# Attention: five of eight diagonal masks put into copies of the gates, and K's low halves gathered in one tile

## The chip, the cores and the metric

The kernel runs on one core of one Trainium2 chip. The metric is device time in microseconds (us) of the whole program. Six things work side by side: TensorE (PE in the profile, with its weight loads shown apart as PEld), VectorE (DVE), ScalarE (ACT), GpSimd (POOL), SyncE (SP), which issues the loads and stores, and the DMA engines that carry them out.

## What is computed

A trunk of two layers over a sequence of 1024 rows of width 1024 in float32. The first layer mixes rows by attention with forgetting gates, the second by gated linear attention, and each is followed by a SwiGLU block. The change touches only the attention of the first layer:

```python
log_f = jax.nn.log_sigmoid(f_logit + b_f)
cum = jnp.cumsum(log_f, axis=1).transpose(0, 2, 1)
scale = FOX_HEAD_DIM ** -0.5
for blk in range(S // Q_BLOCK):                       # 8 blocks of 128 queries
    qs, qe = blk * Q_BLOCK, (blk + 1) * Q_BLOCK
    logits = jnp.einsum('bqhd,bkhd->bhqk', q[:, qs:qe], k[:, :qe]) * scale
    logits = logits + cum[:, :, qs:qe, None] - cum[:, :, None, :qe]
    mask = (qs + jnp.arange(Q_BLOCK))[:, None] >= jnp.arange(qe)[None, :]
    logits = jnp.where(mask[None, None], logits, -jnp.inf)
    p = jax.nn.softmax(logits, axis=-1)
    outs.append(jnp.einsum('bhqk,bkhd->bqhd', p, v[:, :qe]))
```

There are 16 heads of width 64. `cum` is the running sum of the gates' logarithms: each key column carries its own value, and the query's own value drops out in the softmax. In a block of 128 queries only the last 128 keys, the diagonal block, hold pairs to be masked.

## The kernel before

**Layout.** Float32 precision is rebuilt on TensorE from operands split in a high part (float32r, rounded) and a low part (the rest). A projection `mm3` (lines 304 to 307) is three products: high by high, high by low, low by high. Weights stand in the array in tiles of 128 rows by 128 columns, and up to 512 columns stream past them.

**Scores.** Heads go in eight pairs `p`, with `a` = 0 or 1 inside a pair; head h is 2p + a. A unit `(p, a, g)` is one head and two query blocks of 128, qb = 2g and 2g + 1. `scores` (line 1261) does a unit: for each query block it cuts the keys up to the diagonal into one or two parts of at most 512 columns (`cuts`: one part for qb 0 to 3, two for qb 4 to 7), 12 parts in a head. For each part there are

- L1281: a product of Q (128 partitions: the 64 high rows and the 64 low rows, negated and scaled) with K's high half, which stands twice, on both halves of the partitions,
- L1282: a product of the same Q tile with K's low half, which stands on 64 partitions; the other 64 partitions of its tile are zero, so that only Q's high rows count,
- L1284, only for the part that holds the diagonal block: an identity times `maskb` (bf16, 128x128, 1e30 above the diagonal, 0 elsewhere), added into the last 128 columns of the same sum.

The sums stand in PSUM, in one of two buffers (`sr`). DVE then adds the gates' row and takes the minimum in one pass (L1287; signs are turned, so a masked pair is a large positive number). After the parts of a query block ACT takes the exponential with its sum (L1291), DVE the reciprocal (L1292), and POOL scales the rows (L1293). Three tiles per head hold K: `KA` and `KB` (high halves) and `KLA` or `KLB` (low half of the head a = 0 or 1 with its 64 zero partitions).

**Evacuation of K.** `k_evac` (line 863) runs for each half of 512 columns: POOL writes the zeros (L866, L867), ACT makes four copies of the high halves (L868 to L871), DVE subtracts twice for the low halves (L872, L873).

**Gates.** `cum` goes to DRAM once (L1094). `load_cum(h)` (L1106 to L1108) broadcasts a head's row of 1024 values to 128 partitions, into one of two buffers. The first two are loaded in the prologue (`gates_end`), and two more at the end of each pair (L1389, L1390).

**Outputs and order.** `outputs` (line 1296) transposes the scaled rows (L1313), splits them (ACT L174, DVE L175) and multiplies by V (L1325, L1327). A unit's outputs come one unit later than its scores. Within a head the units go in `ORDER` = g 0, 3, 1, 2. While a pair is worked on, `weave` (line 130) threads the next pair's Q and K projections, and half of a group of V, between the scores and outputs by planned costs, and keeps PE's order of the two strands with a lag of 18 yields; after the seventh pair the output projection takes that place. Other steps run in the gaps: weight splits on ACT, POOL and DVE (L242, L246), and the modulation vectors, accumulated on DVE (L505) and POOL (L466, L468) from loads that SP issues (L442). SP works its queue in order: a load that has to wait for its buffer holds up all that stand behind it, the weights (L227) among them.

**Before attention**, in the first microseconds, vectors are turned into columns by transposes of 32, 8 and 16 rows (L1115 and L416) among transposes of 128 rows (L630, L413). In the second layer L331 transposes 128 rows of 16 columns.

**Slots.** SBUF is handed out in slots of 4 KB per partition. The tiles of Q and K take nine: eight, and the slot `s1_sl`, which the prologue uses for modulation weights.

The functions that the change touches:

Of the kernel before, what the change touches and what calls it, by code (L numbers as in the profile page):

```python
# [9 lines left out]
F32 = mybir.dt.float32  # L10
# [43 lines left out]
def trunk(ctx, tc, x, c, ada_w, ada_b, norm1_g, norm2_g, ffn_w_in, ffn_w_out,  # L54
# [768 lines left out]
    vring = Ring(big, take(8))  # L823
    qk_free = deque(take(8) + s1_sl)
    qk_all = list(qk_free)
# [14 lines left out]
    def qk_tiles(p):  # L840


        at = {nm: qk_free.popleft() for nm in ("QA", "QB", "KA")}
        if p:
            before = qk_at.pop(p - 1)
            at.update(zip(("KB", "KLA", "KLB"), (before[nm] for nm in ("QA", "KA", "KLA"))))
            qk_free.extend(before[nm] for nm in ("QB", "KB", "KLB"))
        else:
            at.update({nm: qk_free.popleft() for nm in ("KB", "KLA", "KLB")})
        qk_at[p] = at  # L850
        return {nm: big.tile([P, S], FR, tag=sl, name=f"{nm}{p}") for nm, sl in at.items()}
# [11 lines left out]
    def k_evac(ps, t, hf):  # L863
        cs = hsl(hf)
        KA, KB, KLA, KLB = t["KA"], t["KB"], t["KLA"], t["KLB"]
        nc.gpsimd.memset(KLA[64:128, cs].bitcast(F32), 0.0)  # L866
        nc.gpsimd.memset(KLB[0:64, cs].bitcast(F32), 0.0)  # L867
        nc.scalar.copy(KA[0:64, cs], ps[0:64, :])  # L868
        nc.scalar.copy(KB[64:128, cs], ps[64:128, :])
        nc.scalar.copy(KA[64:128, cs], ps[0:64, :])  # L870
        nc.scalar.copy(KB[0:64, cs], ps[64:128, :])  # L871
        nc.vector.tensor_sub(KLA[0:64, cs], ps[0:64, :], KA[0:64, cs].bitcast(F32))  # L872
        nc.vector.tensor_sub(KLB[64:128, cs], ps[64:128, :], KB[64:128, cs].bitcast(F32))  # L873

# [216 lines left out]
    def gates_end():  # L1091
# [3 lines left out]
        load_cum(0)  # L1095
        load_cum(1)

    def v_split(g, tp, ps):
# [5 lines left out]
    cums = {}  # L1104

    def load_cum(h):  # L1106
        cums[h] = cumr([P, S], F32, f"cum{h}")
        nc.sync.dma_start(cums[h], cum_d[h].partition_broadcast(P))  # L1108

# [151 lines left out]
    def scores(u):  # L1261

        p, a, g = u
        t = qkt[p]
        Qs, K1, KL = (t["QA"], t["KA"], t["KLA"]) if a == 0 else (t["QB"], t["KB"], t["KLB"])
        cm = cums[2 * p + a]
        if g < 2:
            both = lpr([P, (4 * g + 3) * P], F32, f"lp{p}{a}{g}")
# [4 lines left out]
        for qi in range(2):  # L1273
# [3 lines left out]
            for n_, (k0, k1) in enumerate(zip(cuts, cuts[1:])):  # L1277
# [3 lines left out]
                nc.tensor.matmul(ps, Qs[:, qs], K1[:, k0:k1], start=True, stop=False)  # L1281
                nc.tensor.matmul(ps, Qs[:, qs], KL[:, k0:k1], start=False, stop=not diag)  # L1282
                if diag:
                    nc.tensor.matmul(ps[:, k1 - k0 - P:], identb, maskb, start=False, stop=True)  # L1284
                mnew = st[:, qi, n_:n_ + 1]
                with tc.issue_after(v_last) if early else ExitStack():
                    nc.vector.tensor_tensor_reduce(lp[:, k0:k1], ps, cm[:, k0:k1], 1.0, mcur,  # L1287
                                                   ALU.add, ALU.min, mnew)
# [67 lines left out]
    def attention(p):  # L1356
        for a in range(2):
            for g in ORDER:
                u = (p, a, g)
                lps = yield from scores(u)  # L1360
                if p:
                    ada0p(0.8)
# [19 lines left out]
    in_order(begin)  # L1382
    v_last = last_of("D")
    for p in range(7):
        parts = [qk_proj(p + 1, 0), qk_proj(p + 1, 1)]
        if p < 6:
            parts.insert(1, v_half(p // 2 + 1, p % 2))
        weave(attention(p), 23.0, chain(*parts), 31.0 if p < 6 else 20.8, LAGS)
        load_cum(2 * p + 2)  # L1389
        load_cum(2 * p + 3)  # L1390
    ada0.flush()
# [1157 lines left out]
```

## Time and profile before

| | |
|---|---|
| median of 3 runs | 2350.84 us (2349.58 to 2350.93) |
| profiled execution, its own time | 2349.75 us |
| span of its instructions | 2348.0 us |
| mean granted clock of TensorE | 0.995 |
| PE, DVE, ACT, POOL busy, us | 2327.2, 1778.5, 1123.2, 1141.2 |
| products and weight loads | 12168 each |
| first and last product of scores (L1281) start | 97.6 and 589.1 us |
| mask products (L1284) | 128 |

A busy time is the union of recorded durations. Matmuls overlap in the records, since one starts while the one ahead still drains, and their ends are modelled; so the time that a product costs in PE's stream is read from the distance between starts in the timeline. A row of the timeline gives the start, the duration, the engine, the line, the operation, output<-inputs, the weights' size (rows * columns), the shape and type of what streams, how many were merged (x), and in brackets the idle time ahead of it and what ended it. A row of the table by stretches gives a stretch and its length, then the busy time (and count) of PE, PEld, DVE, ACT and POOL, the granted clock, the DMA share and GB/s. In a list of waits stand the waiting line, the line waited for, the total in us, the times and the longest.

### The profile page before, as it was taken

How to read it: one execution, taken by the hardware profiler on the slowest of the kernel's cores; microseconds unless marked ns; L12 is line 12 of the kernel's file. 1: busy time of each engine (PE TensorE's matmuls, PEld its weight loads, DVE VectorE, ACT ScalarE, POOL GpSimd, SP SyncE). 2: the span in 40 equal slices, each digit the busy share in tenths (PEclk: the TensorE clock that was granted, in tenths of full speed). 3: DMA queues.
4: the chain of work that ended last, by engine and by line, in shares of the span. 5: the costliest groups of instructions: out<-in, count | busy, mean ns of one | idle time of the engine just before them, and what ended most of it. 6: DMA issues, size and time to landing. Idle time of an engine off the chain costs nothing.

```text
span 2348.0 us, 35560 instructions
## 1 busy us (share of the span) xinstructions
PE 2327.2 (99%) x12168; PEld 1984.9 (85%) x12168; DVE 1778.5 (76%) x2947; ACT 1123.2 (48%) x2166; POOL 1141.2 (49%) x1005
## 2 busy tenths in 40 slices
PE   8999999999999999999999999999999999999999
PEld 7988888888888888888888899898888888888888
DVE  6578787877688888886788666568787777876787
ACT  6566565675443333344325654345444333345236
POOL 1334445533345656665563522345456666664651
PEclk8999999999999999999999999999999999999999
DMA  8423333332325545458774443555434544458674
GB/s 264 146 77 116 108 115 94 125 129 102 117 95 188 184 162 171 156 174 314 252 270 154 136 127 99 151 171 171 141 111 157 178 149 157 139 188 300 237 264 140
DMA packets 349614, 383.38 MB, mean 163 GB/s; under 512 B 25372, under 2 KB 286648, under 8 KB 349432
## 3 DMA queue, kind: packets, MB, share of 16 engines
q1 hardware_dynamic: 349432, 381.11, 49.4%
q8 instruction: 96, 1.57, 0.3%
q14 instruction: 86, 0.70, 0.1%
HBM read 279.76 MB, written 101.25 MB: 162 GB/s over the span
## 4 chain that ended last, share of the span: by engine, by line
PE 88%; DVE 4%; DMA 3%; issue 1%; ACT 1%; POOL 1%; SPq 1%; DVEq 0%; POOLq 0%; ACTq 0%
PE p_b L305 16%; PE p_b L307 16%; PE p_b L306 16%; PE o_b L1327 2%; PE t_b L1313 2%; PE qk_b L305 2%; PE qk_b L306 2%; PE qk_b L307 2%; PE vps_b L307 1%; PE vps_b L305 1%; PE vps_b L306 1%; PE gv_b L305 1%; PE gv_b L307 1%; PE gv_b L306 1%; PE gr_b L305 1%
## 5 line engine op out<-in xcount | busy, mean ns | idle before, releaser
L174 ACT CAST o_s<-xv_s 128x512 fp32r<-128x512 f32 (+1 forms) x392 | 236.3, 610 | 340.1 <-PE p_b L307 254.3
L175 DVE TENSOR_TENSOR o_s<-xv_s,o_s 128x512 fp32r<-128x512 f32 (+1 forms) x392 | 335.6, 861 | 43.2 <-ACT o_s L174 42.6
L307 PE MATMUL p_b<-B,o_s 128*128 128x512 f32 x608 | 236.0, 389 | 0.0
L306 PE MATMUL p_b<-B,o_s 128*128 128x512 f32 x608 | 235.9, 389 | 0.0
L305 PE MATMUL p_b<-B,o_s 128*128 128x512 f32 x608 | 235.4, 390 | 0.0
L1293 POOL TENSOR_SCALAR lp_s<-lp_s,st 128x128 f32<-128x128 f32 (+7 forms) x128 | 98.0, 769 | 246.0 <-DVE st L1292 227.0
L940 POOL TENSOR_TENSOR ex_s<-xv_s,xv_s 128x512 f32<-128x512 f32 (+1 forms) x64 | 95.1, 1486 | 241.3 <-DMA xv_s<-in_ffn_w_in_dram 119.4
L305 PE MATMUL p_b<-T,o_s 128*128 128x512 f32 x480 | 186.8, 389 | 0.0
L306 PE MATMUL p_b<-T,o_s 128*128 128x512 f32 x480 | 186.7, 389 | 0.0
L307 PE MATMUL p_b<-T,o_s 128*128 128x512 f32 x480 | 181.2, 389 | 0.0
L307 PEld LDWEIGHTS p_b<-B,o_s 128*128 128x128 f32 x608 | 114.1, 188 | 23.9
L305 PEld LDWEIGHTS p_b<-B,o_s 128*128 128x128 f32 x608 | 114.1, 188 | 23.7 <-DVE x L1659 0.2
L306 PEld LDWEIGHTS p_b<-B,o_s 128*128 128x128 f32 x608 | 114.1, 188 | 23.5
L1291 ACT ACTIVATE lp_s<-lp_s,st 128x128 f32<-128x128 f32 (+7 forms) x128 | 99.4, 777 | 58.2 <-DVE st L1287 56.9
L942 POOL TENSOR_TENSOR xv_s<-ex_s,xv_s 128x512 f32<-128x512 f32 (+1 forms) x64 | 94.0, 1469 | 59.1 <-DVE o_s L175 56.0
L1659 DVE TENSOR_TENSOR ex_s<-ex_s,p_b 128x512 f32<-128x512 f32 x140 | 94.2, 681 | 36.7 <-PE p_b L307 36.5
L174 ACT CAST pt_s<-t_b 128x512 fp32r<-128x512 f32 (+1 forms) x160 | 79.7, 547 | 73.6 <-PE t_b L1313 73.0
L246 POOL TENSOR_TENSOR w_l_s<-w__s,w_h_s 128x256 fp32r<-128x256 f32 x90 | 69.3, 799 | 85.9 <-ACT w_h_s L242 67.9
L952 POOL TENSOR_TENSOR xv_s<-xv_s,xv_s 128x512 f32<-128x512 f32 x48 | 65.5, 1365 | 92.2 <-issue 50.4
L175 DVE TENSOR_TENSOR pt_s<-t_b,pt_s 128x512 fp32r<-128x512 f32 (+1 forms) x160 | 96.2, 630 | 15.9 <-ACT pt_s L174 15.4
L307 PEld LDWEIGHTS p_b<-T,o_s 128*128 128x128 f32 x480 | 90.1, 188 | 18.7
L306 PEld LDWEIGHTS p_b<-T,o_s 128*128 128x128 f32 x480 | 90.1, 188 | 18.7
(1527 smaller groups left out, 7415.4 us busy)
## 6 DMA issues: line engine op xcount, KB each, us to landing
xv_s<-in_ffn_w_in_dram SPq DMA_DIRECT2D x176, 256.0 KB, 3.3
hid_B<-x SPq DMA_DIRECT2D x66, 512.0 KB, 2.8
ad_s<-in_ada_w_dram SPq DMA_DIRECT2D x384, 64.0 KB, 2.4
hid_T<-x SPq DMA_DIRECT2D x44, 512.0 KB, 3.0
xv_s<-in_ffn_w_out_dram SPq DMA_DIRECT2D x88, 256.0 KB, 3.6
ada_s<-in_ada_w_dram SPq DMA_DIRECT2D x96, 128.0 KB, 2.8
T2o<-hid_T SPq DMA_DIRECT2D x22, 512.0 KB, 6.6
T1o<-hid_T SPq DMA_DIRECT2D x22, 512.0 KB, 6.5
```

Of the source, the lines that this page charges most:

```text
L174: nc.scalar.copy(hi, src)
L175: nc.vector.tensor_sub(lo, src, hi.bitcast(F32))
L246: (nc.gpsimd if i < 3 else nc.vector).tensor_sub(lo[:, cs], rw[:, cs], hi[:, cs].bitcast(F32))
L305: nc.tensor.matmul(ps, ah, bh, start=start, stop=False, skip_group_check=chain)
L306: nc.tensor.matmul(ps, ah, bl, start=False, stop=False, skip_group_check=chain)
L307: nc.tensor.matmul(ps, al, bh, start=False, stop=stop, skip_group_check=chain)
L940: nc.gpsimd.tensor_add(s1, a21, a22)
L942: nc.gpsimd.tensor_sub(a11, s1, a11)
L952: nc.gpsimd.tensor_sub(r[A12], r[A12], r[A11])
L1291: nc.scalar.activation(lp, lp, AF.Exp, bias=mcur, scale=-1.0, accum_out=st[:, qi, 2:3])
L1293: nc.gpsimd.tensor_scalar(lp, lp, st[:, qi, 3:4], 1.0, op0=ALU.mult, op1=ALU.mult)
L1659: nc.vector.tensor_add(d, d if src is None else dest(G, src), ps)
```

## The change

**Mask in the gates.** Adding the mask to the gates' row before the score pass does what the mask product did. A masked copy is needed wherever the same gates' columns are also used unmasked. Query block 7 is the only reader of the last 128 columns, so there POOL adds the mask in place (`mask_last`). For query blocks 0, 1, 4 and 5 the gates' blocks stand in a new tile of two rows of 512 columns: `dm[0]` holds block 0 (for qb 0) and blocks 0, 1 (for qb 1), `dm[1]` blocks 3, 4 (for qb 4) and blocks 4, 5 (for qb 5), which is the whole key part of that product. `load_near` and `load_far` fill them with two DMAs each per head, and `mask_blocks` adds the mask to the two diagonal blocks of one row in one POOL instruction. Query blocks 2, 3 and 6 keep their mask product. So 80 of the 128 mask products go.

**Order.** For head h + 1, `load_near` is asked for after the first unit's scores of head h, its mask is added after the second unit's; `load_far(h + 1)` and `load_cum(h + 2)` are asked for after the last unit's scores, and the far mask is added ahead of the head's second unit, `mask_last` after its first. The first head's are asked for in the prologue. The two `load_cum` at the end of a pair go.

**K's low halves.** `KLA` and `KLB` become one tile `KL`, head a = 0 on partitions 0 to 63, head a = 1 on 64 to 127. There are no zeros and no memsets; the second product takes only the 64 partitions of Q's high rows and of `KL` (`rows`). That frees the slot `s1_sl`, which the masked copies take.

The diff:

```diff
--- before.py
+++ after.py
@@ -821,7 +821,7 @@
 
     fr = deque(fl)
     vring = Ring(big, take(8))
-    qk_free = deque(take(8) + s1_sl)
+    qk_free = deque(take(8))
     qk_all = list(qk_free)
     cumr = Ring(big, take(2))
     lpr = Ring(big, take(3))
@@ -843,10 +843,10 @@
         at = {nm: qk_free.popleft() for nm in ("QA", "QB", "KA")}
         if p:
             before = qk_at.pop(p - 1)
-            at.update(zip(("KB", "KLA", "KLB"), (before[nm] for nm in ("QA", "KA", "KLA"))))
-            qk_free.extend(before[nm] for nm in ("QB", "KB", "KLB"))
+            at.update(zip(("KB", "KL"), (before[nm] for nm in ("QA", "KA"))))
+            qk_free.extend(before[nm] for nm in ("QB", "KB", "KL"))
         else:
-            at.update({nm: qk_free.popleft() for nm in ("KB", "KLA", "KLB")})
+            at.update({nm: qk_free.popleft() for nm in ("KB", "KL")})
         qk_at[p] = at
         return {nm: big.tile([P, S], FR, tag=sl, name=f"{nm}{p}") for nm, sl in at.items()}
 
@@ -862,15 +862,13 @@
 
     def k_evac(ps, t, hf):
         cs = hsl(hf)
-        KA, KB, KLA, KLB = t["KA"], t["KB"], t["KLA"], t["KLB"]
-        nc.gpsimd.memset(KLA[64:128, cs].bitcast(F32), 0.0)
-        nc.gpsimd.memset(KLB[0:64, cs].bitcast(F32), 0.0)
+        KA, KB, KL = t["KA"], t["KB"], t["KL"]
         nc.scalar.copy(KA[0:64, cs], ps[0:64, :])
         nc.scalar.copy(KB[64:128, cs], ps[64:128, :])
         nc.scalar.copy(KA[64:128, cs], ps[0:64, :])
         nc.scalar.copy(KB[0:64, cs], ps[64:128, :])
-        nc.vector.tensor_sub(KLA[0:64, cs], ps[0:64, :], KA[0:64, cs].bitcast(F32))
-        nc.vector.tensor_sub(KLB[64:128, cs], ps[64:128, :], KB[64:128, cs].bitcast(F32))
+        nc.vector.tensor_sub(KL[0:64, cs], ps[0:64, :], KA[0:64, cs].bitcast(F32))
+        nc.vector.tensor_sub(KL[64:128, cs], ps[64:128, :], KB[64:128, cs].bitcast(F32))
 
 
     def w_loads(wmat, lo, w=P):
@@ -1094,6 +1092,9 @@
         nc.sync.dma_start(cum_d, cum)
         load_cum(0)
         load_cum(1)
+        dm.extend(Views(s1_sl, 2, [HALF], "dm").v)
+        load_near(0)
+        load_far(0)
 
     def v_split(g, tp, ps):
         v = vring([P, 2, 4, 2, 64], FR, f"v{g}{tp}")
@@ -1103,9 +1104,30 @@
 
     cums = {}
 
+    dm = []
+
     def load_cum(h):
-        cums[h] = cumr([P, S], F32, f"cum{h}")
-        nc.sync.dma_start(cums[h], cum_d[h].partition_broadcast(P))
+        if h < 16:
+            cums[h] = cumr([P, S], F32, f"cum{h}")
+            nc.sync.dma_start(cums[h], cum_d[h].partition_broadcast(P))
+
+    def load_near(h):
+        if h < 16:
+            for o, n in ((0, 1), (P, 2)):
+                nc.sync.dma_start(dm[0][:, o:o + n * P], cum_d[h, 0:n * P].partition_broadcast(P))
+
+    def load_far(h):
+        if h < 16:
+            for o, b in ((0, 3), (2 * P, 4)):
+                nc.sync.dma_start(dm[1][:, o:o + 2 * P], cum_d[h, b * P:(b + 2) * P].partition_broadcast(P))
+
+    def mask_blocks(i, b0, n=2):
+        t = dm[i].rearrange("p (b k) -> p b k", k=P)[:, b0:b0 + 3:2]
+        nc.gpsimd.tensor_add(t, t, maskb.unsqueeze(1).to_broadcast([P, n, P]))
+
+    def mask_last(h):
+        t = cums[h][:, 7 * P:]
+        nc.gpsimd.tensor_add(t, t, maskb)
 
 
 
@@ -1262,8 +1284,10 @@
 
         p, a, g = u
         t = qkt[p]
-        Qs, K1, KL = (t["QA"], t["KA"], t["KLA"]) if a == 0 else (t["QB"], t["KB"], t["KLB"])
+        Qs, K1, rows = (t["QA"], t["KA"], slice(0, 64)) if a == 0 else (t["QB"], t["KB"], slice(64, 128))
+        KL = t["KL"]
         cm = cums[2 * p + a]
+        near = {0: (0, 0), 1: (0, P), 4: (1, 0), 5: (1, 2 * P)}
         if g < 2:
             both = lpr([P, (4 * g + 3) * P], F32, f"lp{p}{a}{g}")
             lps = [both[:, 0:(2 * g + 1) * P], both[:, (2 * g + 1) * P:]]
@@ -1279,12 +1303,17 @@
                 early = u == (0, 0, 0)
                 diag = k1 == Wd
                 nc.tensor.matmul(ps, Qs[:, qs], K1[:, k0:k1], start=True, stop=False)
-                nc.tensor.matmul(ps, Qs[:, qs], KL[:, k0:k1], start=False, stop=not diag)
-                if diag:
+                by_pe = diag and qb in (2, 3, 6)
+                nc.tensor.matmul(ps, Qs[rows, qs], KL[rows, k0:k1], start=False, stop=not by_pe)
+                if by_pe:
                     nc.tensor.matmul(ps[:, k1 - k0 - P:], identb, maskb, start=False, stop=True)
+                cmk = cm[:, k0:k1]
+                if diag and qb in near:
+                    i, o = near[qb]
+                    cmk = dm[i][:, o:o + k1 - k0]
                 mnew = st[:, qi, n_:n_ + 1]
                 with tc.issue_after(v_last) if early else ExitStack():
-                    nc.vector.tensor_tensor_reduce(lp[:, k0:k1], ps, cm[:, k0:k1], 1.0, mcur,
+                    nc.vector.tensor_tensor_reduce(lp[:, k0:k1], ps, cmk, 1.0, mcur,
                                                    ALU.add, ALU.min, mnew)
                 mcur = mnew
                 yield max(0.22, 0.00085 * (k1 - k0))
@@ -1355,9 +1384,21 @@
 
     def attention(p):
         for a in range(2):
-            for g in ORDER:
+            h = 2 * p + a
+            for i, g in enumerate(ORDER):
                 u = (p, a, g)
+                if h and i == 1:
+                    mask_blocks(1, 1)
                 lps = yield from scores(u)
+                if i == 0:
+                    if h:
+                        mask_last(h)
+                    load_near(h + 1)
+                elif i == 1 and h < 15:
+                    mask_blocks(0, 0)
+                elif i == 3:
+                    load_far(h + 1)
+                    load_cum(h + 2)
                 if p:
                     ada0p(0.8)
                 if pending[0] is not None:
@@ -1381,13 +1422,14 @@
     run(v_half(0, 1, lambda: split_after.update((e, last_of(e)) for e in "ADG")))
     in_order(begin)
     v_last = last_of("D")
+    mask_last(0)
+    mask_blocks(0, 0)
+    mask_blocks(1, 1)
     for p in range(7):
         parts = [qk_proj(p + 1, 0), qk_proj(p + 1, 1)]
         if p < 6:
             parts.insert(1, v_half(p // 2 + 1, p % 2))
         weave(attention(p), 23.0, chain(*parts), 31.0 if p < 6 else 20.8, LAGS)
-        load_cum(2 * p + 2)
-        load_cum(2 * p + 3)
     ada0.flush()
     ada0p.flush()
```

## The prediction

> **What bounds the kernel now.** I read the page first: span, busy table, clock and the shares of the chain that ended last.
>
> ```profile
> span 2348.0 us, 35560 instructions
> ...
> PE 2327.2 (99%) x12168; PEld 1984.9 (85%) x12168; DVE 1778.5 (76%) x2947; ACT 1123.2 (48%) x2166; POOL 1141.2 (49%) x1005
> ...
> PE 88%; DVE 4%; DMA 3%; issue 1%; ACT 1%; POOL 1%; SPq 1%; DVEq 0%; POOLq 0%; ACTq 0%
> ```
>
> TensorE carries 88% of the chain. The change lies in the attention stage only, so next came the table by stretches for a typical stretch of it, and the list of PE's waits over the stage from 97 to 592 us (five rows; the first and the last).
>
> ```profile
> 225.00:290.00 65.00, 64.73 (x430) 57.21 (x430) 49.35 (x127) 39.59 (x85) 31.40 (x47) 1.00 0.32 99
> ...
> PE t_b L1313 <- POOL lp_s L1293: 2.8, 3, 1.9
> ...
> PE t_b L1313 <- DVE pt_s L175: 0.2, 1, 0.2
> ```
>
> PE is busy 64.73 of 65.00 us at granted clock 1.00, and no wait of PE on another engine adds up to more than 2.8 us over the stage. So here a product that goes or comes counts at what it takes in PE's stream, nearly one for one. What it takes is not its recorded duration (those overlap) but the distance from one start to the next, which the timeline gives. Rows of PE, with the weight loads (PEld) behind them:
>
> ```profile
> 331.20 0.39 PE L306 MATMUL qk_b<-h0l,w_h_s 128*128 128x512 f32 x1
> ...
> 334.17 0.39 PE L307 MATMUL qk_b<-h0h,w_l_s 128*128 128x512 f32 x1
> ...
> 334.57 0.34 PE L1282 MATMUL s_b<-KLB,QB 128*128 128x384 f32 x1
> ...
> 343.24 0.28 PE L1281 MATMUL s_b<-KB,QB 128*128 128x256 f32 x1
> 343.35 0.28 PE L1282 MATMUL s_b<-KLB,QB 128*128 128x256 f32 x1
> 343.48 0.23 PE L1284 MATMUL s_b<-maskb,identb 128*128 128x128 bf16 x1
> 343.52 0.48 PE L306 MATMUL qk_b<-h0l,w_h_s 128*128 128x512 f32 x1
> 343.83 0.28 PE L1327 MATMUL o_b<-pt_s,v_s 128*128 128x256 f32 x1
> ...
> 334.18 0.19 PEld L1281 LDWEIGHTS s_b<-KB,QB 128*128 128x128 f32 x1
> ...
> 334.75 0.10 PEld L1284 LDWEIGHTS <-identb 128*128 128x128 bf16 x1 [0.16 <-issue]
> ```
>
> Between the first two rows lie 13 steps (every row between them is one 512-column product): 2.97 / 13 = 0.23 us per product of 512 columns. One of 256 takes 0.11 (343.24 to 343.35). The load of the next weights starts with the product ahead of it (L1281's at 334.18 beside L307 at 334.17) and so is hidden. The mask's bf16 load is not: it starts at 334.75, which is L1282's start at 334.57 plus the 0.17 that 384 columns stream at the same rate.
>
> **The change, part by part.** *Mask products removed.* From L1282 at 343.35 to the second product behind the mask at 343.83 are 0.48 us. Without the mask it would be 0.11 + 0.23 = 0.34, so a mask product costs 0.14. Five of eight per head go, in 16 heads: 80 x 0.14 = **11.2 us off**, all of it on PE's path. The other 48 stay.
>
> *Second K product over 64 partitions.* How many there are:
>
> ```profile
> L1282 PE MATMUL s_b<-KLA,QA x96: 273/338/415, 97.6 to 559.6; 128*128 128x512 f32 x40, 128*128 128x256 f32 x24, 128*128 128x384 f32 x24, 128*128 128x128 f32 x8
> ...
> L1282 PE MATMUL s_b<-KLB,QB x96: 273/338/448, 128.3 to 589.3; 128*128 128x512 f32 x40, 128*128 128x256 f32 x24, 128*128 128x384 f32 x24, 128*128 128x128 f32 x8
> ```
>
> 192 products. Their column counts stay, so the streaming stays at 0.23 per 512. New is that a product over 64 rows of the array stands between products over 128 rows, 192 times, with a change of row count on each side. The trace has no such product over 64 rows. It has changes of row count at the start, where 32, 8 and 16 rows meet 128:
>
> ```profile
> 4.97 0.28 PE L1115 MATMUL vps_b<-ident,mrows_s 32*128 32x32 f32 x1 [4.97 <-DVE crep L404]
> ...
> 8.00 0.42 PE L413 MATMUL vps_b<-ident,mrows_s 128*128 128x128 f32 x1
> 8.35 0.59 PE L416 MATMUL vps_b<-ident,crep 8*128 8x8 f32 x4
> 8.80 0.37 PE L416 MATMUL vps_b<-ident,mrows_s 16*128 16x16 f32 x2
> 9.10 3.67 PE L630 MATMUL xr_b<-ident,xt_s 128*128 128x128 f32 x16
> ...
> 5.18 0.18 PEld L630 LDWEIGHTS xr_b<-ident,xt_s 128*128 128x128 f32 x1
> ...
> 7.79 0.23 PEld L413 LDWEIGHTS vps_b<-ident,mrows_s 128*128 128x128 f32 x1
> 8.35 0.50 PEld L416 LDWEIGHTS vps_b<-ident,crep 8*128 8x128 f32 x4 [0.33 <-DVE xT L633]
> ...
> 9.10 3.27 PEld L630 LDWEIGHTS xr_b<-ident,xt_s 128*128 128x128 f32 x16
> ```
>
> At all three changes the next load waits until 0.07 us before the recorded end of the product ahead: 4.97 + 0.28 = 5.25 against 5.18; 8.00 + 0.42 = 8.42 against 8.35; 8.80 + 0.37 = 9.17 against 9.10. Where the row count stays it does not wait: L413's load stands at 7.79, 0.21 ahead of its product. (The profile puts 8.35 down to DVE; the crep copies it names at 4.97 are the only input, and the same 0.07 three times speaks for PE.) This is a wait for the product ahead to leave the array, in either direction. In that early stretch a 128-column transpose takes 0.22 (3.67 over 16), so fixed times may be longer there than in attention; I keep the rule "0.07 before the recorded end", which uses attention's own recorded durations.
>
> Its price in attention: the recorded duration of a 512-column product is 0.39, so the load starts 0.32 after the product instead of beside it. That is 0.09 past the 0.23 of streaming; the same difference holds at 384 columns (0.34 - 0.07 - 0.17 = 0.10). Then the load itself is uncovered, which shows where PE restarts after a stop:
>
> ```profile
> 477.52 0.50 PE L305 MATMUL qk_b<-h0h,w_h_s 128*128 128x512 f32 x1 [0.53 <-DVE QB L860]
> 477.86 0.39 PE L306 MATMUL qk_b<-h0l,w_h_s 128*128 128x512 f32 x1
> ```
>
> 0.34 instead of 0.23: an uncovered load costs 0.11. So a change of row count costs 0.09 + 0.11 = 0.20. There are 2 x 192 = 384 of them; at 48 the next product is a mask that stays, whose load is uncovered already, so only the 0.09 counts. Sum: 336 x 0.20 + 48 x 0.09 = **71.5 us on**. Lower bound, if the load waits only for the end of streaming as the mask's does: 336 x 0.11 = 37.0. Upper bound, if it waits for the full recorded end: 336 x 0.27 + 48 x 0.16 = 98.4. Below all that stands no wait at all, 0 (a rival). A gain I exclude: two 64-row products are never neighbours, a 128-row product of the same score stands ahead of each. I take 0.20 because it comes from the three rows that show a change of row count.
>
> The Trainium skill, TensorEngine Tiling (Array Packing), section Tiling Modes, says the same as a rule: "Changing tiling mode (not just tile) drains the TensorE". It gives no time. As a rule about any change of tile shape this trace does not bear it out, as the next rows show.
>
> ```profile
> 1304.71 0.40 PE L307 MATMUL gr_b<-h1h,w_l_s 128*128 128x512 f32 x1
> ...
> 1304.71 0.43 PEld L331 LDWEIGHTS aps_b<-ident,aS 128*16 128x16 f32 x3
> ```
>
> A load of 16 columns over all 128 rows starts with the 512-column product ahead of it and does not wait. So a change of the column count is free; the waits at the start belong to the row count. That leaves doubt whether 64 rows behave as 8 to 32 do, and I keep a quarter of the chance for it.
>
> *POOL.* Out go 32 memsets, in come 32 adds over 256 columns and 16 over 128. The nearest rows:
>
> ```profile
> L866 POOL MEMSET KLA<- x16: 518/519/522, 73.0 to 501.2; 64x512 f32 x16
> ...
> L468 POOL TENSOR_TENSOR acc_s<-acc_s 128x256 f32<-128x256 f32 x31 | 22.9, 739 | 1.4
> ```
>
> -32 x 0.52 + 32 x 0.74 + 16 x (0.37 to 0.74) = +13 to +19 us, on an engine busy 31.40 of 65 us: hidden, unless an add is late for its reader. The tightest is the add on the last block, which stands in POOL's queue behind the two normalisations of the head's first unit and is read by the second part of query block 7. In the tightest head:
>
> ```profile
> 479.96 0.83 POOL L1293 TENSOR_SCALAR lp_s<-lp_s,st 128x128 f32<-128x128 f32 x2
> ...
> 485.89 0.75 DVE L1287 CUSTOM_DVE_ANT_0 lp_s<-s_b,cum_s,st 128x512 f32<-128x512 f32 x1
> ```
>
> The queue is free of them at 480.79, the reader starts at 485.89: 5.1 us for an add of under 0.74. The other two adds have nearly a unit's time or more. Cost nothing; without that cover each late add would hold DVE, with PE behind it through the two score buffers, by its lateness.
>
> *Loads.* Four more DMAs per head, 64 in all, and the gates' load moves from the end of a pair to the end of each head. Each waits on SP's queue until DVE has read the old copy; behind it wait the weight and modulation loads. What such waits cost now:
>
> ```profile
> SPq L1108 <- DVE oT_s L1342: 45.5, 7, 12.6
> ...
> SPq L1108 <- DVE st L1287: 24.8, 6, 9.7
> ...
> DMA to landing us min/median/max: 3.6/4.2/6.1
> ```
>
> The gates' load already holds SP 70.3 us in 13 waits, while PE's waits above come to a few us in all. So I take 0; the bound is one PE stop like the longest above (1.9) per head, 16 x 1.9 = 30 us, and below nothing -2.8, the POOL wait gone. A landing of 4.2 fits: the copies of a head are asked for about a unit or more ahead of their adds. In head 0 they follow the gates' loads at the end of the prologue, ahead of the first score. DVE's score pass reads a copy of the same shape; K's evacuation keeps its six steps. Nothing there.
>
> **Sum.** -11.2 + 71.5 = +60.3 us. The profiled execution took 2349.75 (span 2348.0); the median of the runs is 2350.84, 1.1 more. 2350.84 + 60.3 = **2411**.
>
> **The rivals.** (1) *64-row products pass like any other* (faster). Then only the mask products count: 2350.84 - 11.2 = 2340. For it: the free change of column count, and that the three waits are transposes in plain float32 early on, not products in attention. Against it: three changes, one rule, both directions. It decides at 11.2 / 384 = 0.03 us per change of row count: below that the change gains. The Trainium skill, TensorE: Matmul & The Clock Gate, section "Why this matters for your kernels", has a single product over 32 rows take the same time as one over 128; read as a whole that is this rival's 2340.
> (2) *The load waits only for the end of streaming*: 37.0 - 11.2 = +26, 2377. For it: the mask's load does just that. Against it: the 0.09 past streaming at the start.
> (3) *SP or POOL becomes the wait*: no wait at changes of row count, but each head loses up to 1.9 us on a late copy or late weights: -11.2 + 30 = +19, 2370. For it: 70.3 us of waits on SP at this load already. Against it: the covers above.
> (4) *The two sides cancel*, the wait being about 0.03: near 2351.
>
> **How the numbers follow.** A measurement of this kernel can tell about 0.2% (4.7 us) from no change. Forecast with its bounds 0.58, (2) 0.10, (3) 0.02: slower 0.70. (1) 0.25: faster. (4) 0.05: same. The likeliest case's own range is 2377 to 2438. With a quarter on the other side the range must reach down to rival (1), with the -2.8: 2337. From the top I leave the upper part of the bound out: 2337 to 2430.
>
> **What would show it.** In the profile after: 48 bf16 products instead of 128; rows of 64*128 on L1282's successor; their loads, and the next 128-row loads, starting about 0.32 us after the start of a 512-column product ahead; the product behind with a recorded duration near 0.50; PE distances of about 0.43 around each second product; the attention stage 60 us longer and everything from 660 us on the same length. Loads starting beside the product ahead would prove me wrong and give (1); loads starting 0.23 after it give (2); PE waits on POOL or DVE that grow by tens of us give (3).

## The result and the profile after

The changed kernel takes 2404.45 us (median of 5 runs, 2400.78 to 2406.45) against 2349.58 (5 runs, 2348.46 to 2350.93): a ratio of 1.0231, with a 95% interval of 1.0220 to 1.0242. That is 54.9 us more; the forecast was 60.3 more, 2411.

The profiled execution took 2406.45 us, 2.0 more than the median. From its page, the span, the busy table and the shares of the chain:

```profile
span 2404.7 us, 35567 instructions
...
PE 2385.6 (99%) x12088; PEld 1986.1 (83%) x12088; DVE 1774.7 (74%) x2947; ACT 1124.7 (47%) x2166; POOL 1154.7 (48%) x1021
...
PE 90%; DMA 4%; DVE 3%; issue 1%; POOL 1%; SPq 0%; ACT 0%; POOLq 0%; DVEq 0%; ACTq 0%
```

80 products fewer (12168 before), and yet PE is busy 58.4 us longer. The rows of the second K product, of each Q tile, with shortest, middle and longest duration in ns, first and last start, and below them the idle time that the source view gives:

```profile
L1307 PE MATMUL s_b<-KL,QA x96: 323/442/580, 97.4 to 609.6; 64*128 64x512 f32 x40, 64*128 64x256 f32 x24, 64*128 64x384 f32 x24, 64*128 64x128 f32 x8
...
L1307 PE MATMUL s_b<-KL,QB x96: 322/439/503, 130.7 to 643.0; 64*128 64x512 f32 x40, 64*128 64x256 f32 x24, 64*128 64x384 f32 x24, 64*128 64x128 f32 x8
...
  issue: 38.2, 156
```

The last one started at 589.3 before and starts at 643.0 now, 53.7 us later, and the first at the same place. So the time was added in the attention stage; what follows it is 3.0 us longer (643.0 to 2404.7, against 589.3 to 2348.0). "issue: 38.2, 156" is idle time of the queue of weight loads ahead of L1307, 156 times; the same view of the kernel before lists none for this product (L1282). The timeline of loads shows where it lies now:

```profile
305.55 0.19 PEld L1305 LDWEIGHTS s_b<-KB,QB 128*128 128x128 f32 x1
305.78 0.19 PEld L1356 LDWEIGHTS o_b<-pt_s,v_s 128*128 128x128 f32 x1
306.20 0.18 PEld L1307 LDWEIGHTS s_b<-KL,QB 64*128 64x128 f32 x1 [0.24 <-issue]
306.62 0.19 PEld L306 LDWEIGHTS qk_b<-h0l,w_h_s 128*128 128x128 f32 x1 [0.24 <-issue]
306.73 0.19 PEld L307 LDWEIGHTS qk_b<-h0h,w_l_s 128*128 128x128 f32 x1
...
311.31 0.18 PEld L1307 LDWEIGHTS s_b<-KL,QA 64*128 64x128 f32 x1 [0.36 <-issue]
```

And the products of the same stretch:

```profile
305.77 0.39 PE L1305 MATMUL s_b<-KB,QB 128*128 128x512 f32 x1
306.00 0.28 PE L1356 MATMUL o_b<-pt_s,v_s 128*128 128x256 f32 x1
306.20 0.49 PE L1307 MATMUL s_b<-KL,QB 64*128 64x512 f32 x1
306.63 0.50 PE L306 MATMUL qk_b<-h0l,w_h_s 128*128 128x512 f32 x1
306.96 0.39 PE L307 MATMUL qk_b<-h0h,w_l_s 128*128 128x512 f32 x1
...
310.98 0.40 PE L1305 MATMUL s_b<-KA,QA 128*128 128x512 f32 x1
311.31 0.50 PE L1307 MATMUL s_b<-KL,QA 64*128 64x512 f32 x1
311.74 0.98 PE L1356 MATMUL o_b<-pt_s,v_s 128*128 128x256 f32 x6
```

L1356's load starts at 305.78, with the product ahead of it (305.77). L1307's starts at 311.31, 0.33 after the 512-column product ahead (310.98), 0.10 past its streaming of 0.23. The load behind L1307 waits in the same way: L306's starts at 306.62, 0.42 after the 64-row product (306.20), which had an uncovered load of its own (0.11) to sit out. The product behind that, L307, comes 0.33 after L306: one more uncovered load. So one 64-row product of 512 columns costs 0.10 + 0.20 + 0.10 = 0.40 us beyond its streaming. The heads a = 0 (partitions 0 to 63) and a = 1 (64 to 127) pay the same.

The Trainium skill, TensorEngine Tiling (Array Packing), section Tiling Modes, states that a change of tiling mode drains the TensorE. For changes between 128 and 64 rows the trace agrees: the load waits 0.10 us past the streaming at each.

PE's waits on other engines over the stage, 97 to 650 us, of the changed kernel, and then POOL's waits there:

```profile
PE t_b L1342 <- POOL lp_s L1322: 1.3, 1, 1.3
PE s_b L1305 <- DVE st L1316: 0.9, 2, 0.7
```
```profile
POOL lp_s L1322 <- DVE st L1321: 198.1, 68, 8.6
...
POOL dm_s L1126 <- DMA dm_s<-cum_d: 18.0, 13, 4.7
POOL cum_s L1130 <- DMA cum_s<-cum_d: 17.3, 6, 6.0
```

PE's listed waits fell from 4.8 us to 2.2. POOL's adds do wait for their copies, 35.3 us in all, but PE waits for POOL no more than 1.3 us, less than the 2.8 before.

**An account of the stage.** For the profiled execution of each kernel, the distances from one PE product to the next were added up over the stage (from the first score product to the last second K product), and the streaming (0.227 us for 512 columns, 0.173 for 384, 0.120 for 256) was taken off; what is left is split into the distances beside second K products and masks ("beside scores") and all others ("elsewhere"). The streaming is 463.1 us in each. Where the border between the two is drawn moves an entry by about 1 us.

| kernel | stage, us | beside scores | elsewhere | changes of row count | masks |
|---|---|---|---|---|---|
| before | 491.7 | 28.0 | 0.6 | 0 | 128 |
| changed | 545.7 | 80.4 | 2.2 | 383 | 48 |
| rows_only | 542.2 | 80.1 | -1.0 | 383 | 128 |
| rows_no_mask | 544.3 | 78.5 | 2.6 | 383 | 0 |
| neighbours2 | 535.1 | 59.7 | 12.1 | 255 | 48 |
| gates_only | 505.1 | 24.3 | 17.7 | 0 | 48 |
| gates_ordered | 492.4 | 20.9 | 8.4 | 0 | 48 |
| no_mask5 | 488.8 | 21.6 | 4.1 | 0 | 48 |
| no_mask | 485.3 | 13.4 | 8.9 | 0 | 0 |

The account has one cost in it that is not a product's: the granted clock. In some stretches of the stage it falls to half. In the kernel before there is one, in the changed one two:

```profile
415.80:419.20 3.40, 3.40 (x15) 3.03 (x14) 2.91 (x12) 2.42 (x7) 1.30 (x2) 0.51 0.89 283
```
```profile
449.10:452.50 3.40, 3.40 (x8) 2.35 (x9) 2.81 (x10) 2.12 (x6) 0.48 (x1) 0.50 0.94 295
517.40:520.80 3.40, 3.36 (x9) 2.55 (x9) 1.36 (x7) 0.69 (x3) 2.03 (x4) 0.50 0.86 235
```

PE is busy there, but the distances in each such 3.4 us add up to about 1.6 us more than the streaming. The stage has 3.4 us at half clock in the kernel before, none in rows_only, 6.8 in the changed kernel, rows_no_mask, both gates versions and both versions without masks, and 13.7 in neighbours2. Without the time beyond streaming in these stretches the stage would be 490.0 us before, 542.4 in the changed kernel and 542.2 in rows_only: the last two are then equal within the working.

### The profile page after: what moved, and what is told of

Its sections match the earlier page's. It is cut to its first block, busy times and chain, and to the rows that moved or that the text cites. A ratio compares the mean times of both kernels' runs of the same rounds, so it can differ in the third digit from the quotient of the medians.

```text
span 2404.7 us, 35567 instructions
## 1 busy us (share of the span) xinstructions
PE 2385.6 (99%) x12088; PEld 1986.1 (83%) x12088; DVE 1774.7 (74%) x2947; ACT 1124.7 (47%) x2166; POOL 1154.7 (48%) x1021
## 4 chain that ended last, share of the span: by engine, by line
PE 90%; DMA 4%; DVE 3%; issue 1%; POOL 1%; SPq 0%; ACT 0%; POOLq 0%; DVEq 0%; ACTq 0%
PE p_b L305 15%; PE p_b L307 15%; PE p_b L306 15%; PE s_b L1307 3%; PE o_b L1356 3%; PE t_b L1342 2%; PE qk_b L305 2%; PE qk_b L306 2%; PE qk_b L307 2%; PE s_b L1305 1%; PE vps_b L305 1%; PE vps_b L307 1%; PE vps_b L306 1%; PE gv_b L305 1%; PE gv_b L307 1%
## 5 line engine op out<-in xcount | busy, mean ns | idle before, releaser
L307 PE MATMUL p_b<-B,o_s 128*128 128x512 f32 x608 | 236.0, 389 | 0.0
L306 PE MATMUL p_b<-B,o_s 128*128 128x512 f32 x608 | 235.9, 389 | 0.0
L306 PE MATMUL p_b<-T,o_s 128*128 128x512 f32 x480 | 186.7, 389 | 0.0
L307 PE MATMUL p_b<-T,o_s 128*128 128x512 f32 x480 | 181.2, 389 | 0.0
L307 PEld LDWEIGHTS p_b<-B,o_s 128*128 128x128 f32 x608 | 114.1, 188 | 23.9
L306 PEld LDWEIGHTS p_b<-B,o_s 128*128 128x128 f32 x608 | 114.2, 188 | 23.6
L306 PEld LDWEIGHTS p_b<-T,o_s 128*128 128x128 f32 x480 | 90.1, 188 | 18.7
L307 PEld LDWEIGHTS p_b<-T,o_s 128*128 128x128 f32 x480 | 90.1, 188 | 18.7
L305 PEld LDWEIGHTS p_b<-T,o_s 128*128 128x128 f32 x480 | 90.1, 188 | 18.6
```

What stands on the lines that cost most here:

```text
L305: nc.tensor.matmul(ps, ah, bh, start=start, stop=False, skip_group_check=chain)
L306: nc.tensor.matmul(ps, ah, bl, start=False, stop=False, skip_group_check=chain)
L307: nc.tensor.matmul(ps, al, bh, start=False, stop=stop, skip_group_check=chain)
```

## The experiments

**1. The 64-row products alone (rows_only).** The kernel before, with

```diff
+        rows = slice(64 * a, 64 * a + 64)
-                nc.tensor.matmul(ps, Qs[:, qs], KL[:, k0:k1], start=False, stop=not diag)
+                nc.tensor.matmul(ps, Qs[rows, qs], KL[rows, k0:k1], start=False, stop=not diag)
```

> The kernel before, with one edit: the second K product of each score part takes only the 64 partitions that hold data (its zero tiles, memsets, all 128 mask products and the loads of the gates stay). Theory A, a change of row count makes the next weight load wait about 0.09 us past the streaming and leaves it uncovered for 0.11: of the 384 changes 128 stand ahead of a mask product and cost 0.09, 256 cost 0.20, together +62.7 us, less up to 6 us of PE waits on other engines that this slack takes up: 2406 to 2412 us. Theory B, the slowdown of the change comes from the copies of the gates, their loads and adds: this stays at 2350. Theory C, half and half: about 2380.

Measured: 2399.65 us (4 runs) against 2349.24, ratio 1.0218 (1.0204 to 1.0232), 50.4 us more. This one line carries nearly the whole slowdown. It came out below the 57 to 63 that was expected, and the account says where the difference lies. By the distances of this run's own trace a 64-row product without a mask costs 0.404 beyond streaming and one with a mask 0.42 (from the start of the 64x512 product to the second product behind are 0.762, or 0.779 with a mask between; 0.455 of it is streaming, and 0.097 stands ahead): 64 x 0.404 + 128 x 0.42 = 79.6, and 80.1 was found. In the kernel before 128 masks at 0.137 make 17.5, but 28.0 was found: the other 10.5 us are stops of PE, or distances longer than the usual ones. Distances of more than 0.25 us beyond the streaming make up 7.2 of these; in rows_only they come to 0.7. Its only listed wait of PE on another engine in the stage:

```profile
PE t_b L1314 <- POOL lp_s L1294: 0.2, 1, 0.2
```

**2. The gates alone (gates_only).** The changed kernel with K over 128 partitions again. The nine slots of Q and K then leave none for the copies, so the ring of tiles `pt` goes from four to three.

```diff
-    qk_free = deque(take(8))
+    qk_free = deque(take(8) + s1_sl)
-    ptr = Ring(big, take(4))
+    ptr = Ring(big, take(3))
+    dm_sl = take(1)
...
-                nc.tensor.matmul(ps, Qs[rows, qs], KL[rows, k0:k1], start=False, stop=not by_pe)
+                nc.tensor.matmul(ps, Qs[:, qs], KL[:, k0:k1], start=False, stop=not by_pe)
```

> The changed kernel with the other half undone: masks of five blocks in the gates and their copies, with all their loads and POOL adds, but K's low halves in two zero-padded tiles and products over 128 partitions as before. The copies take a slot from the ring of four tiles of transposed rows, which becomes three. Theory A, only the row count costs: 80 mask products less at 0.13 to 0.14 us each, 10.4 to 11.2 us faster than the kernel before, 2338 to 2340 us, if three tiles of transposed rows are enough. Theory B, the copies cost: slower than 2350, up to 2404.

Measured: 2362.55 us (5 runs), ratio 1.0060 (1.0047 to 1.0074): 13.3 us slower, where 80 products fewer should have made it faster. PE's waits over the stage:

```profile
PE t_b L1344 <- POOL lp_s L1324: 10.5, 8, 4.1
PE s_b L1307 <- DVE st L1318: 4.8, 11, 1.2
```

The longest of them, on POOL's own timeline and then on PE's:

```profile
292.21 0.73 POOL L468 TENSOR_TENSOR acc_s<-acc_s 128x256 f32<-128x256 f32 x1
299.11 0.43 POOL L1133 TENSOR_TENSOR cum_s<-cum_s,maskb 128x128 f32<-128x128 f32 x1 [6.17 <-DMA cum_s<-cum_d]
299.49 0.67 POOL L1129 TENSOR_TENSOR dm_s<-dm_s,maskb 128x256 f32<-128x256 f32 x1
300.14 1.70 POOL L1324 TENSOR_SCALAR lp_s<-lp_s,st 128x768 f32<-128x768 f32 x3
```
```profile
301.10 1.97 PE L1344 MATMUL t_b<-ident,lp_s 128*128 128x128 f32 x8 [4.07 <-POOL lp_s L1324]
```

SP asked for these gates only here:

```profile
292.57 0.34 SPq L1115 DMA_DIRECT2D cum_s<-cum_d  x1
```

POOL stands idle for 6.17 us on an add to gates that were asked for at 292.57, while three normalisations, whose rows PE wants to transpose, stand behind it in POOL's queue. The buffer had just come free from the head that ended, so these are the gates of the head after the one now beginning: nobody needs that add yet. The stop also costs more than its length. PE's granted clock is 0.50 behind it, and 1.00 again from 304.00 on:

```profile
301.10:304.00 2.90, 2.90 (x11) 2.71 (x12) 1.43 (x4) 1.59 (x4) 2.57 (x5) 0.50 0.00 0
304.00:310.00 6.00, 6.00 (x47) 5.61 (x47) 5.62 (x14) 4.50 (x9) 3.14 (x4) 1.00 0.30 93
```

There the three 512-column products from 302.72 on take 0.57, 0.43 and 0.39 us to the next start instead of 0.23. The short ring was the other suspect, so it was run by itself.

**3. The short ring alone (three_pt).** The kernel before with

```diff
-    ptr = Ring(big, take(4))
+    ptr = Ring(big, take(3))
+    spare_sl = take(1)
```

> The control for the run with the gates' half alone: the kernel before, with only the ring of tiles of transposed rows cut from four to three. If three are enough, 2349 us within 2, and the 13 us that the gates' half lost come from the copies themselves. If the short ring is what cost, about 2362.

Measured: 2350.15 us (11 runs) against 2348.83 (21 runs), ratio 1.0006 (0.9997 to 1.0014). The ring costs nothing that can be told from zero.

**4. The adds put in their place (gates_ordered, after_ordered).** gates_only and the changed kernel, with each of POOL's mask adds tied behind the POOL instruction that stands ahead of it in the code:

```diff
-        nc.gpsimd.tensor_add(t, t, maskb)
+        with tc.issue_after(last_of("G")):
+            nc.gpsimd.tensor_add(t, t, maskb)
```

> The gates' half alone again (three tiles of transposed rows, K over 128 partitions), with one edit: each POOL add of the mask is ordered behind the POOL instruction that was written before it, so that it can't stand in POOL's queue ahead of normalisations while it waits for its load. Theory E, the adds that wait for loads at the head of POOL's queue cost the 13 us: back to 2346, that is 80 of 128 mask products at the 5.7 us that leaving out all of them gained, at most 2349. Theory F, the short ring or the loads themselves cost it: stays at 2360 to 2363.

> The changed kernel with the same ordering of the POOL adds, products over 64 partitions as in it. With the row changes PE is late enough to hide most of POOL's waits, so little is to be had: theory E 2400 to 2402, that is the 4.8 us by which the changed kernel is slower than the one with the 64-row products alone, at most; 2404 if that difference has another cause.

Measured: gates_ordered 2352.61 us (11 runs), ratio 1.0017 (1.0009 to 1.0026), so about 10 of the 13.3 us come back; the time stays above the 2346 to 2349 that theory E gave. after_ordered 2401.02 us (4 runs), ratio 1.0224 (1.0210 to 1.0238), against the changed kernel's 1.0231 (1.0220 to 1.0242): not told apart. POOL in the same head of gates_ordered:

```profile
292.86 1.76 POOL L1326 TENSOR_SCALAR lp_s<-lp_s,st 128x768 f32<-128x768 f32 x3 [2.99 <-DVE st L1325]
294.59 0.43 POOL L1135 TENSOR_TENSOR cum_s<-cum_s,maskb 128x128 f32<-128x128 f32 x1
```

The normalisations come first, 7.3 us earlier than in gates_only, and the add that follows, for the head now beginning, does not wait. PE's wait on POOL's rows falls from 10.5 us to 4.3:

```profile
PE t_b L1346 <- POOL lp_s L1326: 4.3, 5, 1.7
```

But the kernel is still not faster than before, with 80 products fewer.

**5. The mask products alone (no_mask, no_mask5).** The kernel before with

```diff
-                diag = k1 == Wd
+                diag = False                              # no_mask
+                diag = k1 == Wd and qb in (2, 3, 6)       # no_mask5
```

> The kernel before without any mask product: all 128 are left out and nothing takes their place, so later keys are not masked. It measures what a mask product is worth in time. If each costs 0.13 to 0.14 us of PE's stream: 16.6 to 17.9 us faster, 2332 to 2333. If the stops of PE on other engines take part of it back: 5 us less than that, 2337. If a mask product costs only its 128 columns of streaming, 0.06 us: 7.7 us faster, 2342.

> The kernel before, with the mask products of query blocks 0, 1, 4, 5 and 7 left out and nothing in their place: no copies, no adds, K over 128 partitions as before. Later keys of those blocks are not masked, so this leaves a part of the computation out. It is the edit that the prediction's 11.2 us term stands for, alone. PE's stream loses 80 products at about 0.13 us, 10.4 us. Theory C (what the version with ordered adds lost, it lost by its copies and adds): nothing is given back, 2338 to 2341. Theory B (the stage is nearly balanced, and PE freed of products waits more for the others, as with all 128 left out, where 14.6 us less around the score products stood beside 8.3 more elsewhere): more than half is given back, 2344 to 2347.

Measured: no_mask 2343.53 us (10 runs), ratio 0.9976 (0.9967 to 0.9986), 5.7 us less; no_mask5 2343.97 (9 runs), ratio 0.9976 (0.9966 to 0.9986), 5.6 less. Leaving out 128 products at 0.137 brings no more that could be told than leaving out 80. For no_mask the time is nearest to the 2342 that was expected if a mask costs its 128 columns of streaming alone (0.06), but the distances speak against that reading: from the start of the second K product to the second product behind it they exceed the streaming by 0.13 us with a mask (middle of the 103 places in the kernel before where no transpose follows) and by 0.01 or less without one (172 places in no_mask). Beside the scores a part of the saving is there: 6.4 us of 11.0 in no_mask5 (28.0 to 21.6) and 14.6 of 17.5 in no_mask (28.0 to 13.4). Elsewhere PE stops more (0.6 to 4.1, and to 8.9), and the half clock takes about 1.6 us more in each. PE's waits in no_mask, on four lines and two engines, none of them large:

```profile
PE t_b L1313 <- DVE pt_s L175: 2.3, 3, 1.6
PE s_b L1281 <- DVE st L1287: 1.9, 6, 0.7
PE qk_b L305 <- DVE QB L860: 1.6, 2, 1.0
PE o_b L1327 <- DVE oT_s L1342: 1.2, 3, 0.5
PE t_b L1313 <- POOL lp_s L1293: 0.6, 2, 0.4
```

So about 5.6 us (3.3 to 8.0 by the interval) is what the change could have gained at best by its masks, with copies and adds for nothing. With them, placed well, it loses: gates_ordered against no_mask5 is 0.0041 of the ratio, about 9.6 us.

**6. Both edits without a mask (rows_no_mask).** rows_only with `diag = False`.

> The kernel before, with the second K product over 64 partitions and all 128 mask products left out (later keys are not masked). Theory I (the two edits share one cost: behind a product over 64 rows the next load is uncovered anyway, so that a mask product there costs its distance alone; from the start of a 64x512 product to the second product behind it are 0.78 us with a mask and 0.76 without): 0.02 us for a mask product, 2 to 4 us less than with the 64 rows alone, so 46 to 49 above the kernel before, 2395 to 2398. Rival (the two edits add up): 128 products at 0.13 us, 17 us less, 2382 to 2385.

Measured: 2401.38 us (4 runs), ratio 1.0214 (1.0200 to 1.0228), against rows_only's 1.0218 (1.0204 to 1.0232). That is above the 2395 to 2398 of theory I, and far from the 2382 to 2385 of its rival. Beside 64-row products 128 mask products are worth nothing that can be measured: the account has 1.6 us less beside the scores, and the trace has 6.8 us at half clock where rows_only has none. The mask's cost was the uncovered load behind it, and behind a 64-row product that load is uncovered anyway.

**7. 64-row products side by side (neighbours, neighbours2).** If the price hangs on changes of row count, putting two 64-row products next to each other halves it. The changed kernel, with both 128-row products of a two-part query block ahead of both 64-row ones; in neighbours2 each 64-row product is also tied behind the PE instruction ahead of it in the code, which keeps other work from coming between:

```diff
-            for n_, (k0, k1) in enumerate(zip(cuts, cuts[1:])):
+            parts, pss = list(zip(cuts, cuts[1:])), []
+            for k0, k1 in parts:
...
+            for ps, (k0, k1) in zip(pss, parts):
...
+                with tc.issue_after(last_of("P")):        # neighbours2
+                    nc.tensor.matmul(ps, Qs[rows, qs], KL[rows, k0:k1], start=False, stop=not by_pe)
```

> The changed kernel with another order of the products: in the query blocks with two key parts both 128-row products come first, then both 64-row products next to each other, so that 64 of the 128-row to 64-row pairs of changes go; numbers of products and columns are the same. Theory A, the price hangs on changes of row count: 128 of 384 changes go at 0.20 us, 25.6 us less than the changed kernel, about 2379, or up to 8 us more where PE has to wait for both score buffers to be free. Theory D, a 64-row product is dearer by itself, about 0.4 us each: no difference, 2404.

> The run with the 64-row products of a query block next to each other, this time with an order that PE keeps: the first of them is tied behind the second 128-row product, and the changes of row count in PE's stream go from 383 to 255. Theory A, the price hangs on the changes: 128 at 0.20 us, 25.6 us less than the changed kernel, 2379; up to 8 us more, 2387, where other engines become late as PE gets faster or PE waits for both score buffers. Theory D, a 64-row product is dearer by itself: 2404.

Measured: neighbours 2402.45 us (4 runs), ratio 1.0227 (1.0214 to 1.0241). It tells nothing: other products were still scheduled between, and there were 369 changes of row count instead of 383. neighbours2 had 255, and took 2394.47 us (4 runs), ratio 1.0191 (1.0176 to 1.0207): about 10 us less, not the 25.6 of 128 changes at 0.20, and 7 above the 2387 of theory A. The timeline of PE in neighbours2 and of its loads:

```profile
312.73 0.39 PE L1304 MATMUL s_b<-KA,QA 128*128 128x512 f32 x1
313.05 0.73 PE L1309 MATMUL s_b<-KL,QA 64*128 64x512 f32 x2
313.71 0.39 PE L1361 MATMUL o_b<-pt_s,v_s 128*128 128x256 f32 x1
```
```profile
313.05 0.29 PEld L1309 LDWEIGHTS s_b<-KL,QA 64*128 64x128 f32 x2 [0.24 <-issue]
313.71 0.53 PEld L1361 LDWEIGHTS o_b<-pt_s,v_s 128*128 128x128 f32 x4 [0.37 <-DVE QB L860]
```

Two 64-row products (x2) take 0.66 us from the change to the next load, where one alone takes 0.42; all 16 such pairs of 512 columns without a mask behind them take 0.66. The second load runs on from the first (0.29 for both), beside the first product, and does not wait; the second product costs its streaming of 0.23 and little else. So the price does hang on the change and not on the 64 rows. The Trainium skill, TensorE: Matmul & The Clock Gate, section The mechanism, has a line by which weight loads overlap with running products only when the row group differs, while the text ahead of that line also lets a load go ahead into the background weight buffer. Here a load overlapped with a product over the same 64 rows, which agrees with the second and not with the first. In the account 20.7 us went beside the scores, and 9.9 came back elsewhere, in waits of PE such as

```profile
PE t_b L1347 <- POOL lp_s L1327: 5.0, 4, 2.8
PE s_b L1304 <- DVE st L1321: 2.8, 6, 0.8
```

With both score buffers taken by one query block before DVE reads the first, such waits are to be expected; that this is their cause was not tried by itself. The half clock, 13.7 us of it against 6.8, took about 4 us of the gain as well.

## Why the prediction was right, and what it had wrong

**The change of row count**: right, in place and size. The loads wait 0.33 after the start of a 512-column product (forecast: about 0.32), the product behind is recorded with 0.50 (forecast: near 0.50), and the starts lie 0.43 apart (forecast: about 0.43). That distance comes once for each lone 64-row product, with 0.33 ahead of it and 0.33 behind; beyond the streaming the three make the same 0.40 as two changes at 0.20. The three transposes over 8 to 32 rows at the start of the program spoke for 64 rows in attention too. They were not all the changes of row count there. A fourth, from 8 to 16 rows, did not wait:

```profile
8.48 0.46 PE L416 MATMUL vps_b<-ident,crep 8*128 8x8 f32 x3
...
8.73 0.33 PEld L416 LDWEIGHTS vps_b<-ident,mrows_s 16*128 16x128 f32 x2
```

The last of the three products ends at 8.94 by its record (8.48 + 0.46), and the load stands at 8.73, 0.21 ahead of that end instead of 0.07. So what the runs bear out is a price for changes between 128 rows and fewer, not for every change of the count. By distances, the 144 products without a mask and the 48 with one make 144 x 0.404 + 48 x 0.42 = 78.3 in the changed kernel against 17.5 for the masks before: 60.8 more. The forecast sum was 60.3. So the mechanism was right, and not only the number.

**"Nearly one for one"**: this is the step that failed. Product time beside the scores grew by 60.8, but 8.4 us of what else stood there went with it (10.5 before, 2.1 after). About half of that can be seen as stops: distances of more than 0.25 us beyond the streaming make 7.2 us beside the scores before and 3.2 after. Most likely a slower PE is waited for by the others instead of waiting for them; no run takes the stops away one by one. 52.4 is left; 1.6 more elsewhere in the stage and 3.0 behind it make 57.0, and the stage begins 0.3 earlier: 56.7 between the spans of the profiled executions. The medians differ by 54.9, since the profiled one of the changed kernel is 2.0 above its median. It fails on the other side as well: of the roughly 11 us that 80 masks take in the stream, 5.6 can be had. The prediction read PE as busy 64.73 of 65.00 us, and the busy time hides stops: records of products overlap, so a short stop can lie under the recorded tail of the product ahead. The list of waits showed 4.8 us; the distances leave 10.5. The busy time also hides the half clock, which PE spends busy.

**The masks' 11.2 us**: right as a distance in the kernel before (0.137 against 0.14), and the sum had the interaction in it, since only the 48 that stay were spared an uncovered load. But read by itself the term misleads: without the row change it is worth about 5.6 at most, with it nothing that can be told (experiment 6).

**POOL's adds at nothing**: right for this kernel, and for a reason that was not given. The cover named was the place in the queue, "behind the two normalisations". gates_only shows that an add can come ahead of them, with a load just asked for, and that it then costs PE stops of up to 4.1 us. In the changed kernel ordering the adds brings nothing that could be told, without the row change about 10 us; most likely the stage, 54 us longer, takes such waits up.

**The loads at nothing**: right here. SP's waits for the buffers of gates and copies are long, and PE's waits fell all the same:

```profile
SPq L1122 <- DVE st L1316: 58.8, 24, 8.9
...
SPq L1112 <- DVE st L1316: 26.6, 11, 3.6
```

In gates_ordered against no_mask5 copies and adds together cost about 9.6; how much of that is loads and how much adds stays open.

**"Everything from 660 on the same length"**: 3.0 us longer after the last score product. The kernels with either part alone have 0.8 and 0.5, after_ordered 1.1, and rows_no_mask is 2.1 shorter there. So executions of these kernels differ by a few us in this part with no order in it, and the 3.0 can't be put down to the change.

**The rivals.** 64-row products do not pass like others: rows_only, with nothing else changed, is 50.4 us slower. The load does not go at the end of streaming but 0.10 later. A wait on SP or POOL is not what made the change slower; POOL's waits are real, but they cost time that could be told only where the row change is undone. No version here that applies all the masks beats the kernel before: the nearest of those that make the change is gates_ordered, 0.17% slower.

## What to carry to other kernels

Where products follow closely, as here, a product over 64 rows among products over 128 is paid for at its borders: count the changes between the two, not the rows, and try whether zero partitions that are left in place cost less. Here the zeros cost no streaming: a second 64-row product of 512 columns beside a first takes 0.24 us (0.66 less 0.42), one over 128 rows 0.23. Setting the small products side by side in pairs got back only about 10 of 55 us. A term read in one neighbourhood (a mask behind a 128-row product) is worth something else in another, so price two edits at the same place together. And in a stage where PE is just the bound, time given to PE and time taken from it do not count alike: test the ceiling first by leaving the work out, which here would have shown 5.6 us before anything was built for it.

## What the runs showed that was not expected

- A 64-row product in a stream of 128-row ones costs 0.40 us at 512 columns beyond its streaming of 0.23, 192 of them 50.4 us; two side by side cost that once.
- A mask product of 128 bf16 columns costs 0.13 to 0.14 us behind a 128-row product and 0.02 behind a 64-row one.
- Leaving out 128 mask products brings 5.7 us, leaving out 80 of them 5.6.
- An add on POOL that waits for a load of its own held up three others behind it, and PE for 4.1 us, though POOL is busy half the time (1171.3 of 2362.5 us in gates_only).
- In gates_only PE ran at a granted clock of 0.50 for the 2.9 us that followed this stop. Stretches of 3.4 us at half clock, 0 to 4 of them in the stage, cost about 1.6 us each, and PE's busy time does not show them.
